# First stage of a hybrid encoder layer: orders written out for three engines, four open value accumulators, constant matmuls between the real ones

## The chip, the cores and the metric

One core of a Trainium2 chip runs the whole layer in one launch. The metric is the device time of that launch in microseconds (us), the median of several runs. The engines are named as the profile names them: PE is TensorE (PEld its weight loads), ACT is ScalarE, DVE is VectorE, POOL is GpSimd, SP issues most of the DMAs.

## What is computed

A layer of width 1024 over 512 positions: a layer norm, one wide projection `w_in` (8 window heads, and three groups of 8 dilated heads, each with q, k and v), two kinds of attention mixed by their softmax denominators, an output projection, a cross attention to a 256-row memory, and a gated feed-forward part, each followed by a residual layer norm. The change touches only the start:

```
h <- LayerNorm(x, ln_in_g, ln_in_b)                 # x is 512 x 1024
z <- h @ w_in;  qa, ka, va, qb, kb, vb = split(z)
# the change: LayerNorm of x, and vb of the first dilated group (512 columns from VB = 3840)
```

## The kernel before, in words

**Precision.** A product of two float32 matrices is made of three matmuls in a faster 32-bit format (`F32R`): each operand is split into a high part (`hi`, a cast on ScalarE, L139) and a low part (`lo = raw - hi`, a subtraction, L141, on VectorE or GpSimd), and hi*hi, hi*lo and lo*hi are summed in PSUM. Weights come by DMA into the tile `raw` (three buffers), and their parts lie in `hi` and `lo` (six buffers each). The transposed activations lie in `Thi` and `Tlo`.

**First stage** (L235 to L358). Rows are taken in four blocks of 128 (`h[0]` to `h[3]`; blocks 0 and 1 lie in tile `oA`, 2 and 3 in `oB`). For each block VectorE takes mean and variance (`stats`, L282, `moments`, L116 and L118), GpSimd the inverse root (L112), VectorE applies gain (L331, `gin` is the gain broadcast) and then shift (L333, `bt` is the bias broadcast, made by two matmuls from the row `brow`), TensorE turns the block in eight 128x128 pieces (`hi_both`, L294), ScalarE casts them to `Thi` (L299), VectorE subtracts for `Tlo` (L327). ScalarE also writes alpha*h to DRAM for the residual (`oW`, L302, L303). Then come the 24 matmuls of that block's values (8 pieces of depth, three products each) into one PSUM tile `g`, copied to `vt` (L341). So the values need 4 x 24 = 96 matmuls of 512 columns; their weights are four pairs of rows, `wv0[0]` to `wv0[3]`, and I call them w0 to w3, and the blocks of the input x0 to x3. Before the first real matmul TensorE multiplies a tile of ones 18 times (`WARM`, L250).

**Order.** Only VectorE's order in this stage is as written (`manual_schedule`). The list `ORDER` sets the order of the loads: x0, gain, w0, x1, w1, w2, x2, x3, w3. w3 must wait for one of the three `raw` buffers. A scheduler with a timeline of its own orders the other engines, and interleaves what follows with the end of the stage.

**What follows.** The projections of the dilated heads: each is a chunk of 24 matmuls into a PSUM tile `g` (two buffers), then a rotation by position (`rope`): VectorE multiplies by `rc` and swaps lanes (L366, L367), GpSimd multiplies by `rsn` and adds (L368, L369). `rc` and `rsn` are sines from ScalarE (L356, L358) of angles that VectorE reduces to one turn (L348 to L357). After three chunks, k0, q0 and the window keys `ka`, comes the first attention item A0, whose first matmuls are `s<-x`. From there on the order of TensorE is written out (`manual_schedule` again).

The memory's rows are also normalised early: `mem_load` (L715, L720) loads gain, bias and rows, and VectorE does the norm on `oB` between the angles.

Of the kernel before, what the change touches and what calls it, by code (L numbers as in the profile page):

```python
# [17 lines left out]
P = 128  # L18
# [30 lines left out]
]  # L49

MEM_AT = (2, 0)
KX = 6
WARM = 18
ORDER = (4, 8, 0, 5, 1, 2, 3, 6, 7)
CI, CF, CS, CMA, CM1, CM3 = 0, 128, 129, 130, 514, 770
CW = 898

# [16 lines left out]
def hymba_layer(ctx: ExitStack, tc: tile.TileContext, A, cst_d, out):  # L74
# [25 lines left out]
    def halves(t):  # L100
        return [t[:, i * 512 : (i + 1) * 512] for i in range(2)]
# [57 lines left out]
    def mm(o, l, r, first, last):  # L159
        nc.tensor.matmul(o, l, r, start=first, stop=last)  # L160
# [26 lines left out]
    def ps_tile(tag, bufs, shape=None):  # L187
        return gpool.tile(shape or [P, 512], F32, tag=tag, bufs=bufs, name=tag)
# [48 lines left out]
    def load_x(b):  # L237
        nc.sync.dma_start(h[b], x2[b * P : (b + 1) * P, :])
# [3 lines left out]
    nc.vector.memset(ones_t, 1.0)  # L242
    brow = wpool.tile([1, D], F32, tag="gb", bufs=2, name="brow")
    nc.sync.dma_start(brow, A["ln_in_b"].partition_broadcast(1))
    ps = ps_tile("t", 1)
    for i in range(WARM):
        mm(ps[:, 0:P], ones_t, ones_t, i == 0, i == WARM - 1)
    sbt = s_tile()
    bt = [sbt[:, n, :] for n in range(2)]
    for n in range(2):  # L250
        mm(bt[n], ones_t[0:1, :], brow[:, n * 512 : (n + 1) * 512], True, True)
    gin = wpool.tile([P, D], F32, tag="gb", bufs=2, name="gin")
    gt = halves(gin)
    wv0 = []
    for u in ORDER:
        if u < 4:
            wv0.append(w_rows(w_in, 2 * u, 2, VB, 512, nc.gpsimd))
        elif u < 8:
            load_x(u - 4)
        else:  # L260
            nc.sync.dma_start(gin, A["ln_in_g"].partition_broadcast(P))
# [14 lines left out]

    hT = T_pair()

    def stats(b):
# [3 lines left out]
        return moments(st)  # L283

    def hi_both(b):
        if b % 2:
            both = s_tile()
            pss = [both[:, i, :] for i in range(2)]
        else:
            pss = [ps_tile("t", 1), ps_tile("o", 1)]  # L290
        out = []
        for i in range(2):
            for k in range(4):
                nc.tensor.transpose(  # L294
                    pss[i][:, k * P : (k + 1) * P], h[b][:, i * 512 + k * P : i * 512 + (k + 1) * P], ident
                )
            hi = hT[0][:, 4 * i : 4 * i + 4, b * P : (b + 1) * P]
            src = pss[i].rearrange("p (k t) -> p k t", k=4)
            nc.scalar.copy(hi, src)  # L299
            out.append((src, hi))  # L300
        ah = oW[:, 2 * (b % 2) : 2 * (b % 2) + 2, :].rearrange("p a f -> p (a f)")
        nc.scalar.activation(ah, h[b], AF.Copy, scale=ALPHA)  # L302
        nc.scalar.dma_start(h_dram[b * P : (b + 1) * P, :], ah)  # L303
        return out

    vt = mkv.tile([P, NB, 512], F32, tag="vm", name="vt")

    def w_v(b, ps, part):
        if b > 1:
            gemm_tm(ps, wv0, hT, blk(b - 1), KX * part, (KX, KD)[part])  # L310
            return
        for k in range(KD):
            whi, wlo = (t[:, k % 2, :] for t in wv0[k // 2])
            if part == 0:
                mm(ps, hT[0][:, k, 0:P], whi, k == 0, False)
                mm(ps, hT[1][:, k, 0:P], whi, False, False)
            else:
                mm(ps, hT[0][:, k, 0:P], wlo, False, k == KD - 1)

    with tc.manual_schedule(engines={nc.vector.engine}):  # L320
        pend = []
        for b in range(NB + 1):
            if b < NB:
                mv, rs = stats(b)
            for i, (ps, hi) in enumerate(pend):
                lo = hT[1][:, 4 * i : 4 * i + 4, (b - 1) * P : b * P]
                nc.vector.tensor_tensor(lo, ps, hi.bitcast(F32), ALU.subtract)  # L327
            if b < NB:
                th = halves(h[b])
                for i in range(2):  # L330
                    nc.vector.scalar_tensor_tensor(th[i], th[i], mv[:, 0:1], gt[i], ALU.subtract, ALU.mult)  # L331
                for i in range(2):
                    nc.vector.scalar_tensor_tensor(th[i], th[i], rs, bt[i], ALU.mult, ALU.add)  # L333
            if b:
                ps = g_tile()
                w_v(b, ps, 0)
            if b < NB:
                pend = hi_both(b)
            if b:
                w_v(b, ps, 1)  # L340
                nc.scalar.copy(vt[:, b - 1, :], ps)  # L341

        rc = cpool.tile([P, S], F32, name="rc")
        rsn = cpool.tile([P, S], F32, name="rsn")
# [366 lines left out]
    def mem_load(b):  # L711
        if b == 0:
            for v in ("mem_ln_g", "mem_ln_b"):
                t = wpool.tile([P, D], F32, tag="gb", bufs=2, name="gm")
                nc.sync.dma_start(t, A[v][0].partition_broadcast(P))  # L715
                gbm.append(halves(t))
            mx = oB[:, 2:4, :].rearrange("p a f -> p (a f)")
        else:
            mx = wpool.tile([P, D], F32, tag="hi", bufs=6, name="mx")
        nc.sync.dma_start(mx, A["mem"].rearrange("o s d -> (o s) d")[b * P : (b + 1) * P, :])  # L720
        mxs[b] = mx

    def mem_T(b, mx):
# [473 lines left out]
```

## Time and profile before

| | |
|---|---|
| median of 3 runs | 975.44 us (975.24 to 977.02) |
| profiled execution, its own time | 976.09 us |
| its span, first to last instruction | 974.0 us |
| busy in the span | PE 95%, DVE 50%, ACT 38%, POOL 21% |
| mean granted TensorE clock | 0.978 of full |

The span is split into 40 slices on the page, so the first stage with the first projections is about the first three of them. A row of the timeline gives start, duration, engine, line, what is written from what, and in brackets the idle time of the engine ahead of it with what ended it. Matmuls overlap: the distance of two starts is what one costs, not its duration. A row of the table by stretches gives a stretch, its length, the busy time of each engine with its instructions, then the granted clock, DMA share and GB/s.

### The profile page before, as it was taken

How to read it: one execution, taken by the hardware profiler on the slowest of the kernel's cores; microseconds unless marked ns; L12 is line 12 of the kernel's file. 1: busy time of each engine (PE TensorE's matmuls, PEld its weight loads, DVE VectorE, ACT ScalarE, POOL GpSimd, SP SyncE). 2: the span in 40 equal slices, each digit the busy share in tenths (PEclk: the TensorE clock that was granted, in tenths of full speed). 3: DMA queues.
4: the chain of work that ended last, by engine and by line, in shares of the span. 5: the costliest groups of instructions: out<-in, count | busy, mean ns of one | idle time of the engine just before them, and what ended most of it. 6: DMA issues, size and time to landing. Idle time of an engine off the chain costs nothing.

```text
span 974.0 us, 12289 instructions
## 1 busy us (share of the span) xinstructions
PE 926.4 (95%) x4825; PEld 770.1 (79%) x4825; DVE 490.2 (50%) x866; ACT 366.4 (38%) x645; POOL 206.4 (21%) x135
## 2 busy tenths in 40 slices
PE   7989999999998899899899997999999999999996
PEld 5777887788776698688887786988888888788885
DVE  6683334524444564749435648454434443333346
ACT  3453444335544557322334512433323332232310
POOL 4253114511443232424541043000000000000001
PEclk7999999999999899999999997999999999999999
DMA  9542032313221227432531034233333333223201
GB/s 320 163 152 65 22 108 66 87 44 108 66 66 47 62 88 214 132 102 58 155 119 44 1 87 130 70 107 104 92 101 95 97 98 98 98 87 108 87 22 65
DMA packets 117066, 93.33 MB, mean 96 GB/s; under 512 B 12471, under 2 KB 100751, under 8 KB 117008
## 3 DMA queue, kind: packets, MB, share of 16 engines
q1 hardware_dynamic: 115106, 90.33, 30.6%
q10 hardware_dynamic: 1902, 2.21, 0.7%
q8 instruction: 38, 0.62, 0.3%
q14 instruction: 20, 0.16, 0.1%
HBM read 88.34 MB, written 4.19 MB: 95 GB/s over the span
## 4 chain that ended last, share of the span: by engine, by line
PE 59%; DVE 5%; ACT 2%; issue 2%; POOL 1%; DMA 0%; DVEq 0%; ACTq 0%; POOLq 0%
PE g L160 25%; PE s L160 15%; PE acc L160 12%; PE t L160 3%; PE o L160 2%; DVE h L129 1%; POOL lo L141 0%; ACT hi L139 0%; DVE lo L141 0%; PE s L206 0%; ACT pu L596 0%; PE t L505 0%; DMA raw<-in_w_xq_dram 0%; PE o L513 0%; DVE ka L704 0%
## 5 line engine op out<-in xcount | busy, mean ns | idle before, releaser
L139 ACT CAST hi<-raw 128x1024 fp32r<-128x1024 f32 x148 | 155.3, 1050 | 249.2 <-PE g L160 161.9
L141 DVE TENSOR_TENSOR lo<-raw,hi 128x1024 fp32r<-128x1024 f32 x114 | 141.7, 1244 | 147.8 <-ACT hi L139 145.7
L141 POOL TENSOR_TENSOR lo<-raw,hi 128x1024 fp32r<-128x1024 f32 x34 | 84.8, 2506 | 121.5 <-ACT hi L139 120.9
L112 POOL TENSOR_TENSOR rs<-ve,mhalf 128x1 f32<-128x1 f32 x18 | 15.6, 868 | 416.6 <-DVE ve L118 416.6
L160 PE MATMUL g<-Thi,hi 128*128 128x512 f32 x240 | 97.6, 407 | 2.1 <-DVE zs L367 2.1
L160 PE MATMUL g<-Thi,lo 128*128 128x512 f32 x240 | 97.0, 404 | 0.0
L160 PE MATMUL g<-Tlo,hi 128*128 128x512 f32 x240 | 96.7, 403 | 0.0
L160 PE MATMUL g<-Ulo,hi 128*128 128x512 f32 (+1 forms) x248 | 91.9, 371 | 1.1 <-DVE Ulo L212 1.0
L160 PE MATMUL g<-Uhi,hi 128*128 128x512 f32 (+1 forms) x248 | 91.7, 372 | 0.6 <-ACT Uhi L211 0.5
L160 PE MATMUL g<-Uhi,lo 128*128 128x512 f32 (+1 forms) x248 | 91.5, 369 | 0.0
L368 POOL TENSOR_TENSOR zs<-zs,rsn 128x512 f32<-128x512 f32 x29 | 57.5, 1983 | 148.4 <-DVE zs L367 148.4
L160 PE MATMUL g<-hi,Thi 128*128 128x512 f32 x200 | 82.7, 414 | 0.5 <-ACT Thi L299 0.3
L160 PE MATMUL g<-hi,Tlo 128*128 128x512 f32 x200 | 81.3, 408 | 1.8 <-DVE Tlo L327 1.8
L160 PE MATMUL g<-lo,Thi 128*128 128x512 f32 x200 | 78.5, 398 | 0.0
L160 PE MATMUL s<-Uhi,hi 128*128 128x512 f32 (+1 forms) x192 | 71.3, 371 | 0.0
L160 PE MATMUL s<-Ulo,hi 128*128 128x512 f32 (+1 forms) x192 | 71.3, 371 | 0.0
L160 PE MATMUL s<-Uhi,lo 128*128 128x512 f32 (+1 forms) x192 | 71.3, 371 | 0.0
L160 PE MATMUL acc<-hi 128*128 128x512 f32 x176 | 68.6, 390 | 0.8 <-DVE act L1117 0.8
L160 PE MATMUL acc<-hi,lo 128*128 128x512 f32 x176 | 68.5, 389 | 0.0
L160 PE MATMUL acc<-lo,hi 128*128 128x512 f32 x176 | 68.5, 389 | 0.0
L160 PEld LDWEIGHTS g<-Thi,hi 128*128 128x128 f32 x240 | 45.8, 191 | 13.5 <-DVE zs L367 2.9
L160 PEld LDWEIGHTS g<-Ulo,hi 128*128 128x128 f32 x248 | 48.8, 197 | 8.7 <-DVE Ulo L212 1.6
(259 smaller groups left out, 1737.4 us busy)
## 6 DMA issues: line engine op xcount, KB each, us to landing
raw<-in_w_in_dram SPq DMA_DIRECT2D x38, 512.0 KB, 3.9
raw<-in_w_gate_dram SPq DMA_DIRECT2D x22, 512.0 KB, 3.8
raw<-in_w_up_dram SPq DMA_DIRECT2D x22, 512.0 KB, 3.9
raw<-in_w_down_dram SPq DMA_DIRECT2D x22, 512.0 KB, 3.3
raw<-in_w_xk_dram SPq DMA_DIRECT2D x8, 512.0 KB, 3.9
raw<-in_w_xv_dram SPq DMA_DIRECT2D x8, 512.0 KB, 3.3
raw<-in_w_xq_dram SPq DMA_DIRECT2D x8, 512.0 KB, 4.1
raw<-in_w_xo_dram SPq DMA_DIRECT2D x8, 512.0 KB, 3.3
```

Of the source, the lines that this page charges most:

```text
L112: nc.gpsimd.tensor_tensor(out_, in_, mhalf, ALU.pow)
L129: nc.vector.scalar_tensor_tensor(th[i], th[i], rs, bt[i], ALU.mult, ALU.add)
L139: nc.scalar.copy(hi, raw)
L141: (eng or nc.vector).tensor_tensor(lo, raw, hi.bitcast(F32), ALU.subtract)
L160: nc.tensor.matmul(o, l, r, start=first, stop=last)
L368: nc.gpsimd.tensor_tensor(sh, sh, rsn, ALU.mult)
```

## The change

Only the first stage is rewritten; line numbers after it are moved by 127, those of the helpers ahead of it by -2.

- **Orders.** TensorE, VectorE and ScalarE all run the stage in the order in which the code stands.
- **Four accumulators.** The values of the four blocks are summed in four PSUM regions that are open at once (`vps`: two `g` tiles and the two halves of an `s` tile). The products hi*hi (`hh`), Tlo*hi (`lh`) and Thi*lo (`hl`) are issued apart.
- **Weights.** The low parts of all four pairs w0 to w3 move from GpSimd to VectorE (`v_lo`). w3 is loaded as two halves into two tiles of another pool, `x`, ahead of x2 and x3.
- **Sums.** Blocks 2 and 3 take their sums on ScalarE (`sums`: part 0 the sum, part 1 the sum of squares about the mean, each one activation over 1024 columns with `accum_out`), and VectorE makes of them the negated mean and the variance (`neg_mean`, `root`).
- **Constants.** The 18 matmuls of ones become 10 ahead of the bias matmuls and 13 behind them, and `busy(3)`, `busy(4)`, `busy(3)` stand at three places between real ones.
- **Transposes** of every block go through the PSUM tiles `t` and `o` (one buffer each).
- **Memory loads** keep the program's order, so they stand behind the weights of the next value group.

```diff
-WARM = 18
-ORDER = (4, 8, 0, 5, 1, 2, 3, 6, 7)
+WARM = (10, 13)
...
-    for u in ORDER:
-        if u < 4:
-            wv0.append(w_rows(w_in, 2 * u, 2, VB, 512, nc.gpsimd))
...
+    def v_raw(i):
...
+        if i < 3:
+            raw = [wpool.tile([P, 2, 512], F32, tag="raw", bufs=3, name="raw")]
+            nc.sync.dma_start(raw[0], src)
         else:
+            raw = [xpool.tile([P, 1, 512], F32, tag="x", bufs=12, name="raw") for _ in range(2)]
+            for k in range(2):
+                nc.sync.dma_start(raw[k], src[:, k : k + 1, :])
...
+    def v_lo(i):
+        for raw, hi, lo in v_parts(i):
+            nc.vector.tensor_tensor(lo, raw, hi.bitcast(F32), ALU.subtract)
+
+    load_x(0)
+    nc.sync.dma_start(gin, A["ln_in_g"].partition_broadcast(P))
+    v_raw(0)
+    load_x(1)
+    for i in range(1, 4):
+        v_raw(i)
+    load_x(2)
+    load_x(3)
...
+    def sums(b, part):
...
+        if part == 0:
+            nc.scalar.activation(junk, h[b], AF.Copy, accum_out=sm)
...
         else:
+            nc.scalar.activation(junk, h[b], AF.Square, bias=LN["nm", b], accum_out=sm)
...
-    with tc.manual_schedule(engines={nc.vector.engine}):
...
+    with tc.manual_schedule(engines={nc.tensor.engine, nc.vector.engine, nc.scalar.engine}):
+        spare = ps_tile("t", 1)
+
+        def busy(n, ps=None):
+            for _ in range(n):
+                mm((spare if ps is None else ps)[:, 0:P], ones_t, ones_t, True, True)
+
+        busy(WARM[0])
+        for n in range(2):
+            mm(bt[n], ones_t[0:1, :], brow[:, n * 512 : (n + 1) * 512], True, True)
+        busy(WARM[1])
+        vps = [g_tile(), g_tile()]
+        two = s_tile()
+        vps += [two[:, i, :] for i in range(2)]
...
+        busy(3, vps[1])
+        hh(0, 0, 1)
+        busy(4, vps[1])
+        hh(0, 2, 3)
+        lh(0, 0, 1, 2, 3)
...
+        sums(2, 0)
+        neg_mean(2)
+        sums(3, 0)
+        turn(1)
+        t_hi(1)
+        v_lo(0)
...
+        turn(3)
+        t_hi(3)
+        v_lo(3)
+        t_lo(3)
+        for b in range(3):
+            hl(b, 6, 7)
+            nc.scalar.copy(vt[:, b, :], vps[b])
+        hh(3, *all_k)
+        hl(3, *all_k)
+        lh(3, *all_k)
+        spill(2)
+        spill(3)
+        nc.scalar.copy(vt[:, 3, :], vps[3])
...
-                nc.sync.dma_start(t, A[v][0].partition_broadcast(P))
+                tc.keep_in_program_order(nc.sync.dma_start(t, A[v][0].partition_broadcast(P)))
```

`turn(b)` is the eight transposes of a block, `t_hi` and `t_lo` its two parts, `gain` and `shift` the two steps of the norm, `spill` the write of alpha*h. Three places of the orders follow; a row is a line of the kernel, the operation, what it writes from what, its shape and how often it stands there in a row.

ScalarE, from the casts of the value weights on to block 2. `hi<-raw` is a cast of weights, `Thi<-` the cast of a turned block, `oW<-` the write of alpha*h. Before:

```order
L139 CAST hi<-raw 128x1024
L302 ACTIVATE oW<-oA 128x1024
L303 DMA h_dram<-oW 128x1024
L299 CAST Thi<-s 128x4x128
L139 CAST hi<-raw 128x1024
L299 CAST Thi<-s 128x4x128
L139 CAST hi<-raw 128x1024 x2
L302 ACTIVATE oW<-oB 128x1024
```

Now, from the sums of blocks 2 and 3 (`zs,sm<-oB`) on; `L137 CAST hi<-raw` is the cast of the weights of k0:

```order
L313 ACTIVATE zs,sm<-oB 128x1024 x2
L354 CAST Thi<-t 128x4x128
L354 CAST Thi<-o 128x4x128
L316 ACTIVATE zs,sm<-oB,nm 128x1024 x2
L363 ACTIVATE oW<-oA 128x1024
L137 CAST hi<-raw 128x1024
L364 DMA h_dram<-oW 128x1024
L354 CAST Thi<-t 128x4x128
L354 CAST Thi<-o 128x4x128
```

The casts of block 1 moved behind the two sums, and a cast of the next stage's weights stands ahead of block 2's.

TensorE, at the transposes of block 2. `g<-hi,Thi` and the like are value matmuls (a written `g` or `s` is the accumulator), `t<-cst` and `o<-cst` transposes. Before, where each block's 24 stand alone:

```order
L294 MATMUL t<-cst,oB 128x128 x4
L294 MATMUL o<-cst,oB 128x128 x4
L160 MATMUL g<-hi,Thi 128x512
L160 MATMUL g<-lo,Thi 128x512
L160 MATMUL g<-hi,Tlo 128x512
L160 MATMUL g<-hi,Thi 128x512
L160 MATMUL g<-lo,Thi 128x512
```

Now, from the transposes of block 2 on, with `lo` the low part of the weights:

```order
L347 MATMUL t<-cst,oB 128x128 x4
L347 MATMUL o<-cst,oB 128x128 x4
L158 MATMUL g<-lo,Thi 128x512 x8
L158 MATMUL s<-hi,Thi 128x512 x8
L158 MATMUL s<-hi,Tlo 128x512 x8
L158 MATMUL s<-lo,Thi 128x512 x4
L158 MATMUL g<-lo,Thi 128x512 x4
L158 MATMUL s<-lo,Thi 128x512 x2
L347 MATMUL t<-cst,oB 128x128 x4
L347 MATMUL o<-cst,oB 128x128 x4
L158 MATMUL g<-lo,Thi 128x512 x4
L158 MATMUL s<-lo,Thi 128x512 x2
```

The matmuls with low weight parts of blocks 0 and 1 stand behind the transposes of block 2, and those of all three blocks around the transposes of block 3.

ScalarE at the end of the stage: the copy of block 3's values, the casts of the next weights and the two sines (`rsn`, `rc`). Before:

```order
L139 CAST hi<-raw 128x1024 x3
L341 COPY vt<-g 128x512
L139 CAST hi<-raw 128x1024
L356 ACT_TABLE_LOAD
L356 ACTIVATE rsn<-zs,cst 128x512
L139 CAST hi<-raw 128x1024
L358 ACTIVATE rc<-zs,halfpi 128x512
```

Now:

```order
L363 ACTIVATE oW<-oB 128x1024
L364 DMA h_dram<-oW 128x1024
L137 CAST hi<-raw 128x1024 x3
L468 COPY vt<-s 128x512
L483 ACT_TABLE_LOAD
L483 ACTIVATE rsn<-zs,cst 128x512
L485 ACTIVATE rc<-zs,halfpi 128x512
```

Three casts of weights now stand together ahead of the last copy, and the sines' table load directly behind it.

More of the change, by code (lines that the diff above doesn't have):

```diff
@@ L277, in hymba_layer @@
     hT = T_pair()
+    vt = mkv.tile([P, NB, 512], F32, tag="vm", name="vt")
+    LN = {}
     def stats(b):
@@ L293, in hi_both, with shift, turn @@
+    def shift(b):
+        th = halves(h[b])
+        for i in range(2):
+            nc.vector.scalar_tensor_tensor(th[i], th[i], LN["rs", b], bt[i], ALU.mult, ALU.add)
+    def turn(b):
+        LN["T", b] = []
+        for i in range(2):
+            ps = ps_tile(("t", "o")[i], 1)
             for k in range(4):
                 nc.tensor.transpose(
-                    pss[i][:, k * P : (k + 1) * P], h[b][:, i * 512 + k * P : i * 512 + (k + 1) * P], ident
+                    ps[:, k * P : (k + 1) * P], h[b][:, i * 512 + k * P : i * 512 + (k + 1) * P], ident
@@ L301, in hi_both, with spill @@
+    def spill(b):
         ah = oW[:, 2 * (b % 2) : 2 * (b % 2) + 2, :].rearrange("p a f -> p (a f)")
@@ L303, in hi_both @@
         nc.scalar.dma_start(h_dram[b * P : (b + 1) * P, :], ah)
[L304 to L318, printed above, removed]
```

144 lines of the change are left out of this document (100 added, 44 removed).

## The prediction

> **What bounds the kernel now.** I read the page first (span, busy shares, clock row), then a table by stretches, then the timeline of the first 70 us.
>
> ```profile
> span 974.0 us, 12289 instructions
> PE 926.4 (95%) x4825; PEld 770.1 (79%) x4825; DVE 490.2 (50%) x866; ACT 366.4 (38%) x645; POOL 206.4 (21%) x135
> PEclk7999999999999899999999997999999999999999
> ```
>
> TensorE is busy 95% of the span, nobody else above 50% (PEld runs beside PE). Idle TensorE time and time at a low clock are thus the whole price of a stage, and the clock row's lowest digits include the first slice.
>
> ```profile
> 0.00:12.20 12.20, 10.02 (x49) 7.79 (x49) 6.07 (x15) 3.59 (x4) 2.69 (x6) 1.00 0.82 270
> 12.20:25.86 13.66, 9.40 (x25) 6.93 (x26) 10.46 (x16) 7.30 (x10) 8.88 (x6) 0.50 0.99 350
> 25.86:44.00 18.14, 16.42 (x78) 12.73 (x77) 11.68 (x19) 6.34 (x10) 0.68 (x2) 1.00 0.67 187
> 44.00:67.70 23.70, 21.07 (x92) 16.79 (x90) 19.47 (x28) 10.18 (x11) 11.91 (x7) 1.00 0.46 146
> 67.70:160.00 92.30, 92.28 (x506) 76.66 (x507) 38.11 (x104) 43.25 (x102) 27.54 (x21) 1.00 0.25 69
> ```
>
> The columns are the stretch, its length, PE, PEld, DVE, ACT and POOL busy, the clock, DMA share, GB/s. From 12.20 to 25.86 TensorE has half its clock and only 25 records. Behind 67.70, where A0 starts, it is busy 92.28 of 92.30 us. So A0's start is the mark: what is done earlier there moves the end.
>
> ```profile
> 1.14 6.29 PE L160 MATMUL t<-zs 128*128 128x128 f32 x36 [1.14 <-DVE zs L242]
> 7.37 1.98 PE L160 MATMUL s<-brow,zs 1*128 1x512 f32 x4
> 9.44 1.41 DVE L333 SCALAR_TENSOR_TENSOR oA<-oA,rs,s 128x512 f32<-128x512 f32 x2 [0.62 <-PE s L160]
> 10.25 0.66 PE L294 MATMUL t<-cst,oA 128*128 128x128 f32 x4 [0.90 <-DVE oA L333]
> 13.09 0.38 SPq L154 DMA_DIRECT2D raw<-in_w_in_dram  x1
> 14.54 4.65 DVE L331 SCALAR_TENSOR_TENSOR oA<-oA,mv,gin 128x512 f32<-128x512 f32 x2
> 19.90 1.12 PE L294 MATMUL s<-cst,oA 128*128 128x128 f32 x4 [1.71 <-DVE oA L333]
> ...
> 67.72 1.95 PE L160 MATMUL s<-x 64*64 64x128 f32 x20 [0.54 <-POOL x L369]
> ```
>
> Three faults show. w3 is asked for only at 13.09. Block 1's gain takes 4.65 us while GpSimd makes low parts beside it. Its transposes come at 19.90 and cost 1.12 us, against 0.66 for block 0's at full clock.
>
> **The change part by part.** Unit prices first.
>
> ```profile
> 1.14:5.36 4.22, 4.22 (x20) 4.22 (x20) 0.29 (x1) 1.28 (x1) 0.00 (x0) 1.00 0.68 194
> 5.36:7.36 2.00, 2.00 (x18) 1.88 (x17) 1.35 (x4) 0.00 (x0) 0.49 (x1) 1.00 0.97 308
> 27.39 0.40 PE L160 MATMUL g<-hi,Tlo 128*128 128x512 f32 x1
> 29.89 0.39 PE L160 MATMUL g<-lo,Thi 128*128 128x512 f32 x1
> ...
> 9.14 1.04 ACT L139 CAST hi<-raw 128x1024 fp32r<-128x1024 f32 x1 [4.63 <-DMA raw<-in_w_in_dram]
> 29.69 1.06 ACT L302 ACTIVATE oW<-oB 128x1024 f32<-128x1024 f32 x1 [3.42 <-DVE oB L333]
> L547 ACT ACTIVATION_READ_ACCUMULATOR pu<-pu,stT 128x1 f32 x32 | 6.0, 187 | 0.0
> 33.52 0.59 ACT L299 CAST Thi<-t 128x512 fp32r<-128x512 f32 x1
> 27.79 1.21 DVE L141 TENSOR_TENSOR lo<-raw,hi 128x1024 fp32r<-128x1024 f32 x1
> 34.15 0.69 DVE L327 TENSOR_TENSOR Tlo<-t,Thi 128x512 fp32r<-128x512 f32 x1 [1.86 <-ACT Thi L299]
> 35.35 1.41 DVE L331 SCALAR_TENSOR_TENSOR oB<-oB,mv,gin 128x512 f32<-128x512 f32 x2
> ```
>
> A constant matmul is two passes: 4.22/20 = 0.21 us each to 5.36, about 0.11 behind it, so the full clock came near 5.4. From 27.39 to 29.89 lie 11 steps: a 512-column matmul costs 0.227 us (at half clock 0.427). A gain alone on VectorE is 1.41.
>
> *Loads.* Their order decides when weights and rows are there.
>
> ```profile
> 3.38 2.06 SPq L154 DMA_DIRECT2D raw<-in_w_in_dram  x2
> DMA to landing us min/median/max: 3.9/6.5/8.2
> ...
> 6.90 0.85 SPq L238 DMA_DIRECT2D oB<-in_x_dram  x2
> DMA to landing us min/median/max: 7.7/8.1/8.4
> ```
>
> The upper pair is of `raw` (w1, w2 and later weights), the lower of x2 and x3. w2 is issued near 5.1 and lands near 13.3; x2 at 6.9+7.7 = 14.6, x3 at 7.4+8.4 = 15.8: one 512 KB piece each 1.3 us. w3 now takes x2's place: w3 14.6, x2 15.9, x3 17.1.
>
> *Start and constants.* 10 constants: 20 x 0.21 = 4.3, to 5.4. Bias: four passes of 0.43, to 7.1, so block 0's shift loses its 0.62 wait. 13 constants: 26 x 0.11 = 2.9, to 10.0, where the transposes start (10.25 before). The other ten stand where TensorE waits for a cast: block 0's at 11.2 to 13.3, block 1's at 17.8; I cost them at nothing, and at most 10 x 0.22 = 2.2 without that cover.
>
> *Block 0.* ScalarE casts the block to 11.8, then w1, w2, w3 as they land, the last to 15.4; the last four matmuls follow: 16.4. VectorE's gain for block 1 is 1.41, not 4.65, and its shift is done at 16.2; transposes 16.4 to 17.7.
>
> *Block 1.* Here the change adds waits to ScalarE's queue: the sums of x2 (15.9, 1.06 + 0.19 = 1.25) and x3 (17.1 to 18.3) stand ahead of block 1's casts. No row has a 1024-column sum: it lies between 1.06 with a free read-out and 1.44 with one that takes twice as long; I take the sum of the two nearest rows. Two of the four are on the path, so 0.4 us either way. So those run 18.3 to 19.5, TensorE waits 1.1 us, and block 1's 16 high-part matmuls end at 22.6. VectorE has the four low parts now, 4 x 1.21 = 4.8 us, but none of the two blocks' statistics.
>
> *Block 2.* Squares on ScalarE to 20.6, then on VectorE gain 1.41 (22.0), w1's low part 1.21 (23.2), half a shift 0.7 (23.9). TensorE waits 1.3 us more; transposes to 25.2.
>
> *From there* TensorE has 34 matmuls, the transposes of block 3 (1.3), 6, then 22 of k0, block 3's 24, and 26 that end k0 and q0: 112 x 0.227 + 1.3 = 26.7, to 51.9. Beside it VectorE finishes block 3's shift near 30, so its transposes at 33 don't wait; low parts of k0 and q0 (2.4) and then of block 3 are done by 35.4, as k0 starts.
>
> *Rotation.*
>
> ```profile
> 53.25 1.28 ACT L356 ACT_TABLE_LOAD   x1
> 55.98 0.72 ACT L356 ACTIVATE rsn<-zs,cst 128x512 f32<-128x512 f32 x1 [1.45 <-DVE zs L355]
> 60.06 0.68 DVE L366 TENSOR_TENSOR zs<-g,rc 128x512 f32<-128x512 f32 x1
> 60.67 0.72 DVE L367 STREAM_SHUFFLE zs<-g 128x512 f32<-128x512 f32 x1
> 61.44 0.50 PE L160 MATMUL g<-Thi,hi 128*128 128x512 f32 x1 [2.11 <-DVE zs L367]
> 61.53 1.29 POOL L368 TENSOR_TENSOR zs<-zs,rsn 128x512 f32<-128x512 f32 x1 [9.38 <-DVE zs L367]
> 62.90 2.16 POOL L369 TENSOR_TENSOR x<-zs 128x512 f32<-128x512 f32 x1
> 84.56 0.69 DVE L476 COPY va<-t 128x512 f32<-128x512 f32 x1 [6.59 <-PE t L475]
> ```
>
> Before, the third chunk waits 2.11 us at 61.44 for k0's PSUM buffer, since the rotation starts late. Now the sines stand behind three weight casts and block 3's copy, which TensorE releases at 44.5 and 45.9: casts to 47.5, copy 48, table 49.3, two sines 50.7, VectorE 0.68 + 0.72 to 52.2. TensorE waits 0.3 to 0.6 there, 24 matmuls (5.45) bring it to 57.8. GpSimd does k0 and q0 from 52.2 in four steps of 1.29 to 2.16, near 58. So A0 starts at 58.1 against 67.72.
>
> *Memory norm.* It moves behind A0's reductions on VectorE and costs some 4.5 us there (two statistics, 1.41 + 1.41, the rest). VectorE's idle 6.59 us ahead of 84.56 hides it; without that cover it would be 4.5 late.
>
> **Sum.** 67.7 - 58.1 = 9.6 us. On the profiled execution's own time: 976.09 - 9.6 = 966.5; that run lies 0.65 above the median of 975.44, so 965.8. My chain carries some 30 steps of handing over between engines at an estimated 0.05 us, so it may be short by 1; later falls of the clock (the 8 and the 7 in the clock row) shift against the program and may add or save one piece at half clock, 1.5 to 2 us by estimate.
>
> **The rivals.**
>
> *The full clock comes late.* In the timeline it came near 5.4, about as the 10th constant ends. Had it not come then, the bias would cost 3.4 and 13 constants 5.5 us: transposes at 14.4, not 10.0. ScalarE's waits for w1 to x3 take up some 1.6 of this, leaving 2.7: 968.5. For it speaks that only 10 constants stand ahead of bias matmuls of one row; against it, that this run's clock rose within them. The Trainium skill, "TensorE: Matmul & The Clock Gate", Part 1, has the full clock follow a whole busy window of about 3.4 us, the windows running free of the kernel's start: a run of 4.3 us holds a whole one in a quarter of the phases by estimate, so by that rule alone 968.5 would be the forecast and not 965.8. The rise near 5.4 agrees with it for this one phase; whether a one-row matmul counts as busy no run here shows. From the rows, I give it 22%.
>
> *ScalarE stands behind k0's weights.* Their cast is queued ahead of block 2's casts; the load can start only when VectorE has w0's low part (18.4) and is wanted at 22.7. With the 3.9 us of the row it is hidden; with the median 6.5 or the 8.2, 1.7 to 3.4 us are lost: 967.5 to 969.2. The long ones fall in the stretch of DMA share 0.99, and at 18.4 all early loads have landed, so I take the short end. A fall of the clock near 25, after 2.7 us in which TensorE has only transposes, would cost as much (one or two pieces of 3.4 us at half clock). 13% together.
>
> *Slower: the clock stays at half.* Before, it fell at 12.2 behind transposes and stayed for 13.66 us although TensorE was busy for 9.40 of them. Each matmul at half clock costs 0.2 more; 48 of them eat the 9.6 us, all 118 up to block 3's end would give 965.8 + 23.6 = 989. Against it: from 25.2 on TensorE has 112 matmuls without a wait, and before the clock returned after some 3 us of such work. 3%.
>
> *Hidden anyway.* A0 comes earlier but something fixed holds the rest: 975.4. The 92.28 of 92.30 speaks against it. 3%.
>
> **How the numbers follow.** The likeliest case, 965.8 with its own range 963 to 967.5, has 57%; the late clock 22%, ScalarE's wait or a fall 13%, hidden 3%, slower 3%, and 2% for a larger gain than I see. The range of 962.5 to 970.5 leaves out the last three. A measurement here can tell 0.2%, 2 us, from no change: faster by more 0.93, within 0.03, slower 0.04.
>
> **What the profile after would show.** `s<-x` starts near 58; full clock from about 5 on without a stretch like 12.20 to 25.86; block 1's gain 1.4 us; TensorE waiting about 1 us each for block 1's casts and block 2's shift; the 2.11 us at the third chunk below 1. Wrong would make me: transposes of block 0 behind 12, a cast of k0's weights that waits over 2 us with block 2's casts behind it, or TensorE waits behind A0 that weren't there.

## The result and the profile after

The changed kernel takes 970.79 us (median of 20 runs, 969.66 to 975.6), the kernel before 976.65 us in the same series (20 runs from 974.93). Two disturbed runs are in no ratio: one of the kernel before (1052.2 us), and the profiled one of the repeat in experiment 1 (4691.44 us), which thus left no second profile to read. The ratio is 0.9949, 95% interval 0.9935 to 0.9962: faster by 5.0 us by the ratio and by 5.9 between the medians, about half of the 9.6 us forecast, and the time is 0.3 us outside the range. The profiled execution took 973.17 us.

The page after, its span, its busy shares and its clock row:

```profile
span 971.3 us, 12351 instructions
PE 929.1 (96%) x4855; PEld 774.5 (80%) x4855; DVE 486.9 (50%) x867; ACT 370.5 (38%) x654; POOL 199.9 (21%) x131
PEclk9999999999999899899999997999999999999999
```

The 7 that stood for the first slice is a 9. The table by stretches of the changed kernel (the columns are those of the table of before), cut at block 0's and block 2's transposes, at the third chunk and at A0:

```profile
0.00:12.10 12.10, 10.90 (x51) 9.34 (x51) 6.16 (x15) 2.33 (x2) 0.75 (x5) 0.86 0.82 270
12.10:25.05 12.95, 11.53 (x69) 9.86 (x69) 10.26 (x19) 11.54 (x18) 2.00 (x2) 1.00 0.63 223
25.05:53.22 28.17, 27.71 (x129) 22.50 (x129) 18.35 (x29) 14.01 (x19) 6.30 (x4) 1.00 0.59 171
53.22:61.32 8.10, 5.70 (x24) 4.39 (x24) 6.86 (x10) 4.65 (x5) 7.89 (x4) 1.00 0.80 233
```

From 12.10 to 25.05 TensorE now has the full clock and 69 records, 20 of them constants, where before it had half the clock and 25 in about the same time. (The clock column counts the time ahead of the clock's first record, 4.87 here, as full, though a constant takes 0.21 us there as before.) The holes that are left: a clock of 0.86 ahead of 12.10, 1.42 us idle at block 2, and 2.40 us in the last stretch, in which GpSimd is busy for 7.89 of 8.10 us. The timeline of TensorE, the rows that answer to those shown of before:

```profile
1.14 4.26 PE L158 MATMUL t<-zs 128*128 128x128 f32 x20 [1.14 <-DVE zs L240]
5.33 1.98 PE L158 MATMUL s<-brow,zs 1*128 1x512 f32 x4
7.24 4.80 PE L158 MATMUL t<-zs 128*128 128x128 f32 x26
12.10 0.66 PE L347 MATMUL t<-cst,oA 128*128 128x128 f32 x4
...
25.05 0.63 PE L347 MATMUL t<-cst,oB 128*128 128x128 f32 x4 [1.42 <-issue]
...
53.22 0.47 PE L158 MATMUL g<-Thi,hi 128*128 128x512 f32 x1 [0.39 <-DVE zs L494]
61.32 0.87 PE L158 MATMUL s<-x 64*64 64x128 f32 x10 [2.40 <-POOL x L496]
```

A0 starts at 61.32 (forecast 58.1, before 67.72). The 26 constant records behind the bias take 4.80 us, not 2.9. And behind A0, the kernel before and then the changed one, from A0 to the end:

```profile
67.72:974.00 906.28, 869.53 (x4585) 725.87 (x4585) 442.50 (x792) 338.98 (x613) 182.28 (x116) 0.98 0.29 87
```

```profile
61.32:971.00 909.68, 873.30 (x4585) 728.43 (x4585) 445.29 (x798) 338.00 (x612) 182.93 (x117) 0.98 0.29 88
```

The same 4585 matmuls take 3.4 us longer. So the profiled execution was short of its forecast by 3.2 us ahead of A0 and by 3.4 to 3.7 behind it.

### The profile page after: what moved, and what is told of

Read it like the earlier page. It is cut to its first block, busy times and chain, and to the rows that moved or that the text cites. A ratio compares the mean times of both kernels' runs of the same rounds, so it can differ in the third digit from the quotient of the medians.

```text
span 971.3 us, 12351 instructions
## 1 busy us (share of the span) xinstructions
PE 929.1 (96%) x4855; PEld 774.5 (80%) x4855; DVE 486.9 (50%) x867; ACT 370.5 (38%) x654; POOL 199.9 (21%) x131
## 4 chain that ended last, share of the span: by engine, by line
PE 59%; DVE 5%; ACT 2%; issue 2%; POOL 1%; DMA 0%; DVEq 0%; ACTq 0%; POOLq 0%
PE g L158 25%; PE s L158 15%; PE acc L158 12%; PE t L158 3%; PE o L158 2%; DVE h L127 1%; POOL lo L139 0%; ACT hi L137 0%; DVE lo L139 0%; PE s L204 0%; ACT pu L723 0%; PE t L632 0%; DMA raw<-in_w_xq_dram 0%; PE o L640 0%; DVE ka L831 0%
## 5 line engine op out<-in xcount | busy, mean ns | idle before, releaser
L137 ACT CAST hi<-raw 128x1024 fp32r<-128x1024 f32 x144 | 151.1, 1051 | 243.7 <-PE g L158 152.6
L139 POOL TENSOR_TENSOR lo<-raw,hi 128x1024 fp32r<-128x1024 f32 x30 | 76.0, 2549 | 123.2 <-ACT hi L137 122.6
L158 PE MATMUL g<-hi,Thi 128*128 128x512 f32 x184 | 73.1, 407 | 0.2 <-DVE h L1117 0.2
L158 PE MATMUL g<-lo,Thi 128*128 128x512 f32 x184 | 71.7, 401 | 0.0
L158 PE MATMUL g<-hi,Tlo 128*128 128x512 f32 x184 | 71.2, 399 | 0.0
L493 DVE TENSOR_TENSOR zs<-g,rc 128x512 f32<-128x512 f32 x29 | 20.0, 690 | 70.8 <-PE g L158 35.2
```

Source lines behind the costliest of these rows:

```text
L137: nc.scalar.copy(hi, raw)
L139: (eng or nc.vector).tensor_tensor(lo, raw, hi.bitcast(F32), ALU.subtract)
L493: nc.vector.tensor_tensor(zc, ps, rc, ALU.mult)
```

## The experiments

All medians are of several runs, with the ratio to the kernel before in the same series and its interval. "A0" is the start of `s<-x`. Each median is to be compared with the changed kernel's 970.8.

### 1. The bias over 128 rows (bias128), and the changed kernel again (a_again)

```diff
-    brow = wpool.tile([1, D], F32, ...)
-    nc.sync.dma_start(brow, A["ln_in_b"]...)
+    brow = wpool.tile([P, D], F32, ...)
+    nc.gpsimd.memset(brow, 0.0)
     load_x(0)
+    nc.sync.dma_start(brow[0:1, :], A["ln_in_b"]...)
-    mm(bt[n], ones_t[0:1, :], brow[...], True, True)
+    mm(bt[n], ones_t, brow[...], True, True)
```

> The changed kernel once more, for a second profile and more times. Theory 'clock': the granted clock rises after the first constants, falls again while the one-row bias matmuls run (they don't count as work for the clock), and how much of the 13 constants then runs at half clock depends on where the clock's 3.41 us steps fall in this run: transposes of block 0 between 9.7 and 14.4 us, 12.1 in the first profile. Theory 'GpSimd': the first attention item waits for GpSimd's rotation of q0 (2.40 us at 61.3 in the first profile) in every phase, here 1.5 to 2.6 us. Rival: the wait of 2.4 us was an accident of that run and is below 0.6 here. Time 970 to 975, as the 20 runs.

> The bias row is laid into a tile of 128 rows, the others zero, and the two bias matmuls contract over all 128 rows instead of one; the result is the same. Theory 'clock': the array counts as busy all along, so the clock, once up, does not fall before 12 us, the 26 passes of the 13 constants take 0.11 us each (2.9 in all, not 4.8), and block 0's transposes start near 10.1, not 12.1; the first attention item comes up to 2 us earlier than in the first profile of the changed kernel (59.3 against 61.3), and the median falls by 1 to 2 us. Rival: the clock falls for another reason (always in the window after its first rise): same fall, transposes near 12, no change in time.

Again: 970.69 us over five runs, ratio 0.9943 (0.9925 to 0.996). What was expected of its profile has no answer from this run; but in the five other profiles that keep this rotation and this place of A0 (bias128, fill, lo_pool, stats_dve, no_busy) A0 waits 2.34 to 2.37 us, so the 2.40 was no accident of one run. With 128 rows: 969.74 us, 0.992 (0.9907 to 0.9934); the two intervals overlap. TensorE's timeline with 128 rows:

```profile
1.14 3.84 PE L158 MATMUL t<-zs 128*128 128x128 f32 x20 [1.14 <-DVE zs L240]
6.46 1.95 PE L158 MATMUL s<-brow,zs 128*128 128x512 f32 x4 [1.48 <-DMA brow<-in_ln_in_b_dram]
8.26 3.06 PE L158 MATMUL t<-zs 128*128 128x128 f32 x26
11.38 0.66 PE L348 MATMUL t<-cst,oA 128*128 128x128 f32 x4
```

The same 26 constants take 3.06 us in place of 4.80. The clock's records show why: its stretches are multiples of 3.41 us, which I call windows. In the changed kernel the clock rose at 4.87, fell at 8.28 and rose again at 11.69. With 128 rows it rose at 4.0 and stayed up for 58 us. The first window behind the rise, in the changed kernel and then with 128 rows:

```profile
4.87:8.28 3.41, 3.41 (x18) 2.04 (x17) 1.91 (x5) 0.00 (x0) 0.55 (x1) 1.00 0.95 319
```

```profile
4.00:7.41 3.41, 1.93 (x12) 1.29 (x11) 2.55 (x6) 0.51 (x1) 0.55 (x1) 1.00 0.98 310
```

TensorE is busy throughout the first, but for more than half of it (5.33 to 7.24) with matmuls over one row, and the clock fell at its end. It is busy for only 1.93 us of the second, and the clock stayed. So the one-row matmuls don't keep the clock up: this is the mechanism of my first rival, in another place. About 1.7 us come back at the constants; the row now lands later (a wait of 1.48), so block 0's transposes gain 0.7 and A0 0.8 (60.54). The median gains 1.0, which the intervals can't tell from nothing.

### 2. The rotation of k0 and q0 on VectorE (rope_dve), and both (bias_rope)

```diff
-        nc.gpsimd.tensor_tensor(sh, sh, rsn, ALU.mult)
-        nc.gpsimd.tensor_tensor(view[1](dest), ...)
+        eng = nc.vector if rn[0] < 3 else nc.gpsimd
+        eng.tensor_tensor(sh, sh, rsn, ALU.mult)
+        eng.tensor_tensor(view[1](dest), ...)
```

> The rotation's product and sum for k0 and q0 run on VectorE instead of GpSimd (four instructions). Theory 'GpSimd': its four steps of 1.3 to 2.3 us in a row, stretched by VectorE's low parts beside them, are what the first attention item waits for; on VectorE they take 0.6 to 0.7 each and the wait is gone (below 0.4 us), the item starts 2 to 2.4 us earlier (about 59), and the fall of the clock near 63 (it costs 1.3 us) goes too: 2 to 3.5 us off the median, 967 to 969. Rival: VectorE is as late, or TensorE then waits as long for something behind it: 970 to 971.

> Both edits. If the two costs add up, the first attention item starts near 57.3 and the median is 965.5 to 968. If they hide each other (the item waits for one chain only), it is no better than the better of the two alone.

970.05 us, 0.9935 (0.9915 to 0.9954), and 969.33 us, 0.9918 (0.9899 to 0.9937). The waits of TensorE with the rotation on VectorE:

```profile
60.13 1.95 PE L158 MATMUL s<-x 64*64 64x128 f32 x20 [1.52 <-DVE x L497]
```

and VectorE's timeline there:

```profile
54.76 0.74 DVE L494 STREAM_SHUFFLE zs<-g 128x512 f32<-128x512 f32 x1
55.39 2.34 DVE L139 TENSOR_TENSOR lo<-raw,hi 128x1024 fp32r<-128x1024 f32 x2
57.65 0.69 DVE L496 TENSOR_TENSOR zs<-zs,rsn 128x512 f32<-128x512 f32 x1
58.25 1.22 DVE L139 TENSOR_TENSOR lo<-raw,hi 128x1024 fp32r<-128x1024 f32 x1
59.39 0.69 DVE L497 TENSOR_TENSOR x<-zs 128x512 f32<-128x512 f32 x1
```

The wait fell from 2.40 to 1.52 only, because the scheduler put three low parts of later weights (3.5 us) between q0's swap and its sum. So most of the wait moved from GpSimd's queue to VectorE's. The fall of the clock near 63 is gone in both profiles, but neither time can be told from that without the edit (970.05 against 970.8, 969.33 against 969.74 of bias128): the 2 to 3.5 us of the theory did not come, and the two edits together ended above their 965.5 to 968.

### 3. A0 twelve matmuls later (later)

```diff
-        ready[key] = now[0] + LAG
+        ready[key] = now[0] + (LAG if rn[0] > 2 else 36)
```

> The changed kernel with A0 let in 36 matmuls behind k0 and q0 and not 24, so that 12 matmuls of the fourth chunk, which stood behind A0's group, stand ahead of it; no other row of TensorE moves. Theory (A0 waits 2.40 us for GpSimd's four rotation steps, which end at 61.3, and nothing else is late): the 12 matmuls (2.7 us) run in the wait, which falls to 0 to 0.2; the fall of the clock near 63 goes too (1.3 us); median 966.5 to 968.5. Rival (the fourth chunk's weight is as late as the rotation, or the later parts of the chain bind): the wait stands ahead of the 12 matmuls, 970 to 971.

968.74 us, 0.9908 (0.989 to 0.9926). TensorE's row of A0:

```profile
61.48 1.95 PE L158 MATMUL s<-x 64*64 64x128 f32 x20
```

A0 starts at the same time, but waits for nothing, and 12 matmuls of the fourth chunk lie behind it already; the fall near 63 is gone. The theory holds: 2.0 us by the medians, though 968.74 lies 0.2 above its range. Nothing else was late at A0.

### 4. Who makes GpSimd's steps long (lo_wait)

The steps that A0 waits for, on GpSimd in the changed kernel, and the low parts on VectorE beside them:

```profile
53.22 1.31 POOL L495 TENSOR_TENSOR zs<-zs,rsn 128x512 f32<-128x512 f32 x1 [0.72 <-DVE zs L494]
54.60 2.16 POOL L496 TENSOR_TENSOR x<-zs 128x512 f32<-128x512 f32 x1
56.73 2.34 POOL L495 TENSOR_TENSOR zs<-zs,rsn 128x512 f32<-128x512 f32 x1
59.14 2.13 POOL L496 TENSOR_TENSOR x<-zs 128x512 f32<-128x512 f32 x1
```

```profile
54.21 1.39 DVE L139 TENSOR_TENSOR lo<-raw,hi 128x1024 fp32r<-128x1024 f32 x1
56.69 1.23 DVE L139 TENSOR_TENSOR lo<-raw,hi 128x1024 fp32r<-128x1024 f32 x1 [1.09 <-ACT hi L137]
58.07 2.07 DVE L139 TENSOR_TENSOR lo<-raw,hi 128x1024 fp32r<-128x1024 f32 x1 [0.16 <-ACT hi L137]
```

The edit holds these three low parts back until q0's sum has ended:

```diff
-        (eng or nc.vector).tensor_tensor(lo, raw, hi..., ALU.subtract)
+        part = (eng or nc.vector).tensor_tensor(lo, raw, hi..., ALU.subtract)
+        # three low parts on VectorE, those behind the third chunk's:
+        tc.add_manual_dep(part.ins, <q0's sum>, Sync)
```

> The changed kernel with the three low parts that VectorE makes behind q0's product and shuffle held back until GpSimd has ended q0's sum. Theory (GpSimd's steps are long because VectorE's low parts run beside them): the four steps, 1.31, 2.16, 2.34 and 2.13 us in the changed kernel, come down to some 1.3 each, the last ends at 58.6 to 59, TensorE's wait of 2.40 falls to 0 to 0.4 and the fall of the clock near 63 goes: 967.5 to 969; a new wait of the fourth chunk for its low part up to 1 us. Rival (the steps have their lengths by themselves, or by what they read): still 8 us from 53.2 to 61.3, the wait of 2.4 stays and the low parts come 2 us later on top: 971 to 973.

974.92 us, 0.9977 (0.9967 to 0.9988). GpSimd, with the low parts held back:

```profile
52.60 1.30 POOL L505 TENSOR_TENSOR zs<-zs,rsn 128x512 f32<-128x512 f32 x1 [0.71 <-DVE zs L504]
53.98 1.29 POOL L506 TENSOR_TENSOR x<-zs 128x512 f32<-128x512 f32 x1
55.23 1.30 POOL L505 TENSOR_TENSOR zs<-zs,rsn 128x512 f32<-128x512 f32 x1
56.61 1.30 POOL L506 TENSOR_TENSOR x<-zs 128x512 f32<-128x512 f32 x1
```

TensorE in the same run:

```profile
58.23 1.95 PE L168 MATMUL s<-x 64*64 64x128 f32 x20
...
66.10 0.33 PE L645 MATMUL t<-cst,pu 128*128 128x128 f32 x1 [1.61 <-ACT pu L687]
67.96 0.97 PE L645 MATMUL t<-cst,pu 128*128 128x128 f32 x3 [1.53 <-ACT pu L687]
```

On the mechanism the theory was right to a tenth: the four steps take 1.30 each, and A0 starts at 58.23 with no wait, where the prediction had put it (58.1). Of the 3.1 us that A0 comes earlier, 0.6 are this execution's start, in which the clock did not fall (GpSimd's first step at 52.60 and not 53.22). On the time it was wrong: 974.92 lies above both ranges. The low parts now stand ahead of A0's reductions on VectorE, A0's transposes wait 1.61 and 1.53 us for the exponentials, the clock falls for 3.4 us at 68.0, and by 72 us into the span TensorE is 0.5 us behind the changed kernel. So VectorE's 3.5 us of low parts must run beside something here; the cheap way is to let GpSimd be slow and give TensorE other work, as in experiment 3. The Trainium skill, "SBUF — State Buffer", section "Who interferes with whom", says that a VectorE instruction with two inputs in SBUF and a GpSimd instruction that reads SBUF exclude each other, and that the one that comes second waits for the whole of the other. The trace agrees: the steps are 1.3 or about 2.15 with nothing between (2.34 where two low parts touch one step), and the third low part itself takes 2.07 in place of 1.22.

### 5. Parts undone: low parts on GpSimd (lo_pool), statistics on VectorE (stats_dve), no constants between (no_busy)

```diff
# lo_pool, in v_lo
-            nc.vector.tensor_tensor(lo, raw, ...)
+            nc.gpsimd.tensor_tensor(lo, raw, ...)
# stats_dve: sums(2, ·), neg_mean(2), root(2) -> stats(2); the same for block 3
# no_busy
-        busy(3, vps[1])
-        busy(4, vps[1])
-        busy(3, vps[2])
```

> The changed kernel with the low parts of the four value weights made by GpSimd again, where VectorE made them. Theory (two engines working beside each other on these rows slow each other, as in the kernel before, where the gain took 4.65 us beside GpSimd's low parts): block 2's gain and shift, 2.8 us alone, stretch to 6 or more and TensorE's wait for block 2 grows from 1.4 to 4 or more; A0 2.5 to 4 us later than 61.3, 973 to 975. Rival (VectorE had too much to do, and each low part taken off it is 1.22 us won): A0 at 60 to 61.3, 969.5 to 971.

> The changed kernel with the statistics of blocks 2 and 3 made by VectorE's own statistics instructions (1.29 + 0.21 + 0.15 us for a block) and no sums or squares on ScalarE. Theory (VectorE is what TensorE waits for at block 2): VectorE's queue grows by 1.65 us ahead of block 2's gain, while ScalarE's casts of block 1 start 1.2 us earlier; the wait for block 2 (1.42) grows to 2 to 3, A0 0.5 to 1.5 us later, 971 to 972.5. Rival (ScalarE binds, its 5 us of sums stand ahead of every cast): A0 1 us earlier, 969 to 970.

> The changed kernel without the ten constant matmuls between block 0's and block 1's matmuls (2.2 us of TensorE). Theory (they hold the clock up): in the windows of 3.4 us between 11.7 and 22 TensorE then has work for only half the time, the clock falls for one to three windows, each costs 1 to 1.4 us, A0 1 to 4 us later: 972 to 975. Rival (they cost time or do nothing): 970 to 971, the clock row as it was.

Low parts on GpSimd: 973.67 us, 0.9981 (0.9964 to 0.9998), 2.9 more; block 2's transposes come at 26.80. The theory's direction holds, its sizes don't: block 1's gain takes 3.56 and block 2's 2.07 in place of 1.41, but the wait is 2.01 in place of 1.42, not 4 or more, and A0 comes 1.8 later (63.08), not 2.5 to 4. By the ratios as they stand, over half of the gain is gone without this part.

Statistics on VectorE: 972.55 us, 0.9953 (0.9939 to 0.9967). The wait at block 2 is 2.58, as the theory had it, and in this profile the clock falls at 25.9; A0 comes at 63.76. The ratio can't be told from the changed kernel's, so what the sums on ScalarE are worth in time isn't shown.

No constants between: 972.01 us, 0.9947 (0.9929 to 0.9965), no difference that can be told, and the clock did not fall from 13.6 to 64.8. The ten constants show no effect here; that is one profile, whose clock rose late. This profile shows something else, the forecast's first rival as it was written:

```profile
1.14 4.63 PE L158 MATMUL t<-zs 128*128 128x128 f32 x20 [1.14 <-DVE zs L240]
5.70 3.78 PE L158 MATMUL s<-brow,zs 1*128 1x512 f32 x4
9.41 5.15 PE L158 MATMUL t<-zs 128*128 128x128 f32 x26
14.62 0.66 PE L347 MATMUL t<-cst,oA 128*128 128x128 f32 x4
```

Here the clock rose only at 13.6: bias 3.78 us, transposes at 14.62 (the rival said 3.4 and 14.4), A0 at 63.77. The code up to block 0's transposes is the changed kernel's. Where the windows lie differs from execution to execution: in eight profiles with the one-row bias and ten constants ahead of it the first rise came at 4.2 to 5.5 in six, at 6.5 in one (lo_wait) and at 13.6 in one. The six fell again at 7.6 to 8.9. The one at 6.5 did not fall: 1.5 us of its window were one-row matmuls, less than half, and block 0's transposes came at 11.23.

### 6. Both repairs, with the row's wait covered (bias_later)

Experiments 1 and 3 together, and `WARM = (16, 5)` in place of `(10, 13)`.

> The changed kernel with the bias matmuls over 128 rows (as in the run of that name), 16 constant matmuls ahead of them, so that TensorE doesn't wait for the row, and 5 behind; and A0 let in 36 matmuls behind k0 and q0. Theory: the two gains add up: the row's wait of 1.48 us is covered, transposes of block 0 near 9.3 in place of 12.1, and the start 0.7 to 1.7 us shorter, A0's wait gone: 966 to 968. Rival (the early transposes only wait for w1 to w3, and the gain of the start was the clock's alone): 967.5 to 968.7. Rival two (with another start the clock may rise a window later, at 9 to 13): 969 to 971.

964.75 us, 0.9873 (0.9855 to 0.989): 12.4 us below the kernel before, 6.0 below the changed one and 1.2 below the theory's range, the fastest of all. The table by stretches, cut at the same events:

```profile
0.00:9.53 9.53, 8.33 (x46) 7.19 (x46) 4.41 (x12) 2.18 (x2) 1.71 (x6) 1.00 0.79 254
9.53:23.91 14.38, 11.93 (x68) 9.96 (x69) 12.16 (x23) 12.00 (x19) 2.00 (x2) 1.00 0.75 270
23.91:52.09 28.18, 27.72 (x129) 22.51 (x129) 18.36 (x29) 14.05 (x19) 6.30 (x4) 1.00 0.55 163
52.09:60.43 8.34, 8.34 (x37) 6.65 (x37) 6.62 (x9) 3.76 (x4) 8.00 (x5) 1.00 0.83 234
```

Transposes at 9.53 and block 2 at 23.91; from 52.09 to A0 TensorE has no idle time. With the 12 matmuls moved (2.7 us) A0 stands 3.6 us earlier in the work than in the changed kernel. Between the two profiled executions, 964.84 and 973.17 us, the other 4.7 lie behind A0, where this one has 23.9 us at half clock and the changed kernel 34.1.

### 7. The low clock behind A0 (fill, before_fill, best, fill592)

In eight profiles of kernels whose code behind A0 is the same, the time from A0 to the end goes with the time at half clock behind A0, read from the clock's records (the stretch that runs into the end is left out, and so is lo_wait, 37.5 and 914.6, where three low parts moved behind A0):

| kernel | half clock behind A0, us | A0 to end, us |
|---|---|---|
| bias_rope | 20.5 | 904.6 |
| rope_dve | 23.9 | 906.4 |
| before | 27.3 | 906.3 |
| stats_dve | 27.3 | 907.3 |
| no_busy | 27.3 | 907.5 |
| lo_pool | 30.7 | 908.5 |
| bias128 | 34.1 | 908.9 |
| changed | 34.1 | 910.0 |

A line through them has a slope of 0.34 us for each us (correlation 0.96), 1.2 us for each window of 3.41. The executions of one kernel go the same way: over 65 of the kernel before, time and granted clock have a correlation of -0.86. And the traces show the places. The lead of the changed kernel, from the starts of the same TensorE record in both traces, is 6.4 us at A0 and 4.8 behind its fall at 62.9, which the kernel before doesn't have. It is still 4.8 at 314, 4.4 behind falls near 300 and 330 that both have, 2.0 behind three falls at 377 to 404 where the kernel before has one, 3.5 behind a fall at 473 that only the kernel before has, and 2.6 from 608 on, where transposes stand in another order and TensorE waits 0.68 and 0.22 us that the kernel before doesn't wait. So some 2.9 of the lost 3.8 us go where the clock is low, and 0.9 at that wait.

The first try to take these falls away put constants into the later waits:

```diff
+    def fill(o, n):
+        for _ in range(n):
+            mm(o, ident, ident, True, True)
# ahead of the memory's transposes 13 and 19, of the statistics' 5, of the `rh` pairs 2 and 5, in to_T 17
```

> The changed kernel with constant matmuls (128x128, two passes, 0.22 us at full clock) put on TensorE into its later waits: 13 and 19 ahead of the memory transposes (waits of 3.31 and 4.64 us), 5 ahead of the statistics' transposes (1.28), 2 and 5 ahead of the pairs that read `rh` (0.53, 1.38, 1.38) and 17 ahead of the last transposes of the second norm (4.20). Theory: behind A0 the time hangs on the stretches at half clock; over the five profiles so far A0 to end is 904.6, 906.4, 906.3, 908.9 and 910.0 us with 20.5, 23.9, 27.3, 34.1 and 34.1 us at half clock. The 30.6 us from 301 to 602 go, A0 to end falls by 0.3 to 0.4 of that, 9 to 12 us, to 898 to 901, and the median from 970.8 to 959 to 962. Rival, the matmuls in the waits only stand in the way: no gain, or 0.2 to 0.5 us lost for each place, 971 to 974.

> The kernel before with the same constant matmuls at the same places. Theory (what is missing behind A0 is the place of the half-clock stretches, not the work): A0 stays at 67.7, A0 to end is that of the changed kernel with the same matmuls within 1 us (898 to 901), and the two medians differ by the 6.4 us of A0 less the fall near 63 (1.3), so by 5 to 6.4. Rival (the change itself makes something behind A0 slower, by a transfer or a buffer): A0 to end is 2.5 to 4 us shorter here than in the changed kernel with the matmuls, and the medians differ by 2.5 to 4.

> The changed kernel with all of this together: the bias row in a zeroed 128-row tile loaded over ScalarE's queue, so that its matmuls contract over 128 rows, 7 constant matmuls behind them and not 13; A0 let in 36 matmuls behind k0 and q0; the constant matmuls in the later waits. Theory: transposes of block 0 near 9.9, the clock up from 4 on, no wait of A0; start 1 us, A0 3 to 3.7 us, later stretches 9 to 12 us: 955 to 958. Rivals: the early transposes wait for w1 to w3 anyway, so that the start brings 0: 956 to 959; the places interfere and only the later stretches count: 959 to 962.

979.76 us (1.0024, 1.0013 to 1.0036), 985.58 us (1.0083, 1.0068 to 1.0099) and 976.06 us (0.9985, 0.9973 to 0.9998). The first two are 9 us slower than the same kernels without the constants, and the third is 14 us above the highest of its ranges, which neither theories nor rivals had. TensorE in the changed kernel with the constants, its constants and the memory's transposes:

```profile
294.86 3.07 PE L159 MATMUL t<-cst 128*128 128x128 f32 x26
297.77 0.60 PE L864 MATMUL t<-cst,oB 128*128 128x128 f32 x4
302.07 0.79 PE L864 MATMUL t<-cst,oB 128*128 128x128 f32 x4 [1.88 <-DVE x L869]
```

The wait is at the second four transposes, and my constants stood at the first, where they only took their 3 us; the 17 went to a block that doesn't wait. So these three runs don't settle what the low clock costs: in the first two the time at half clock behind A0 fell by 6.8 us, but the constants took more. They do say that the kernel before and the changed one differ by the same with the constants as without (5.8 us by the medians), as before_fill's theory had it. In the two profiles A0 to the end is 2.8 us shorter in the kernel before (913.7 against 916.5), as its rival had it, with 6.8 us less at half clock. In the third, the row went over ScalarE's queue, came at 7.3, and the clock rose at 13.4.

The second try put 17 constants exactly into the longest wait, 4.2 us near 588, on top of experiment 6:

```diff
+            tc.keep_in_program_order(nc.tensor.matmul(ps[:, 0, 0:P], ident, ident, ...))
# to_T of blocks 1 to 3 written behind block 3's product, 17 constants ahead of block 1's
```

> The kernel of the run before with the bias over 128 rows, 16 and 5 constant matmuls and the later A0, and 17 constant matmuls (3.7 us at full clock) directly ahead of the transposes of the second norm's block 1, behind the last matmul of its product, where TensorE waits 4.2 us for VectorE and the clock then is at half for 10.2 us in nearly all profiles. Theory (behind A0 the time hangs on the stretches at half clock, 0.35 us for each us by the spread of nine profiles): the 10.2 us go, 3 to 3.6 us shorter, 961 to 962. Rival (the matmuls only fill time and the half clock costs little there, since TensorE waits for other engines in it): 964 to 965.5.

967.69 us, 0.9895 (0.9879 to 0.9912). From 583 to 600, without the constants (experiment 6) and then with them:

```profile
583.00:600.00 17.00, 13.57 (x78) 12.77 (x79) 14.00 (x24) 4.27 (x7) 3.05 (x3) 0.70 0.54 164
```

```profile
583.00:600.00 17.00, 13.64 (x99) 12.44 (x97) 14.31 (x25) 3.67 (x6) 4.21 (x3) 0.90 0.62 185
```

The half clock shrank from 10.2 to 3.4 us there, as meant, and the time did not: it is no shorter than experiment 6's (the intervals overlap), and 967.69 lies above the rival's range too. The traces show two effects. From the last matmul of the product (580.26 in experiment 6, 581.41 here) until the next 48 matmuls (`g<-U`) and the 16 transposes that stand among or behind them are through, 18.9 us pass in experiment 6 and 17.5 here. But the edit also moved those transposes behind the 48 matmuls, and then TensorE waits 0.68 and 0.23 us for ScalarE and VectorE, which it doesn't in experiment 6. So 6.8 us less at half clock brought some 1.3 us here, less than the slope of the table, since TensorE waits for other engines in part of this stretch, and the order took most of it back. No experiment removes the low clock behind A0 alone. That most of the 3.4 us is lost there is read from the traces; why the falls come where they do in one execution and not in another stays open.

## Why the prediction was wrong

**Right.** That A0's start carries the gain; block 1's gain of 1.41, and the wait of 2.11 at the third chunk down to 0.39. From block 2's transposes to the end of the 112 matmuls it had 28.0 us (23.9 to 51.9), and 27.8 were measured (25.05 to 53.22 less the wait of 0.39). The sums on ScalarE took 1.06 to 1.17 with 0.18 to 0.20 for the read-out, where it had 1.25. k0's weights delayed ScalarE's queue by 0.36. The memory norm cost nothing: the lead over the kernel before stays at 4.7 to 4.8 us from 68 to 300. The fall near 25 was seen in one profile (statistics on VectorE), not in the changed kernel's.

**The step "start and constants"** failed: 13 constants took 4.80 us, not 2.9, and block 0's transposes came at 12.10, not 10.0, which the prediction itself had named as a sign of being wrong (behind 12). The rival had the right mechanism (a one-row matmul may not count as work) but only as a late rise; what came in most profiles was a rise, a fall at about 8 and a second rise. Of the 2.1 us only 1.15 reach block 2 (25.05 against 23.9), because waits that the prediction had on the way vanished: ScalarE casts w1 to w3 in a row (13.75 to 16.8) and waits for none of them, and TensorE doesn't wait the forecast 1.1 us for block 1's casts. Experiment 6 gives the 1.15 back: 23.91. By the rule of the Trainium skill, "TensorE: Matmul & The Clock Gate", Part 1, a busy window of about 3.4 us brings the full clock, and the windows run free of the kernel's start. The first rises, at 4.2 to 13.6 with the same code ahead of them, agree with the second half. The rise at 4.0 in bias128 came behind a window (0.59 to 4.0) that was busy for 2.86 us, so it need not be a whole one. That one-row matmuls don't count is not in that rule; experiment 1 shows it.

**The step "rotation"** failed most. I took GpSimd's four steps about as before (1.29, 2.16, 1.29, 1.28: 6.0 us). They took 7.94, since the earlier stage brings VectorE's low parts of the next weights right beside them. Of the span "1.29 to 2.16" that I quoted I priced little more than the lower end. TensorE was ready at 58.92 (57.8 forecast, the 1.1 from the start again) and A0 waited to 61.32. Experiment 3 shows that this wait with the fall behind it was worth 2.0 us; experiment 4 shows its cause, and that taking the cause away gives a wait in its place.

**The term "1.5 to 2 us" for later falls** was too small for the profiled execution: 3.4 us behind A0, with two falls more than before. In the 20 runs of the changed kernel 13 lie at 969.66 to 971.23 (granted clock 0.981 to 0.984) and 7 at 972.8 to 975.6 (0.977 to 0.983); the profiled one is of the upper group.

By the medians the miss is 5.0 us. The forecast started from a median of three runs, 975.44; in the series of the result the same kernel takes 976.65, so 1.2 of the 5.0 are no fault of the working, and without them the time would have lain inside the range: that it lies outside by 0.3 is in part bad luck. The two steps above failed all the same. Ahead of A0 the profiled execution misses 3.2 us, 1.1 by the start and the rest by the rotation. The two repairs bring 6.0 us by the medians (964.75), but in the profiles only 3.6 of the 8.3 us lie ahead of A0. How much of the rest is where the clock's windows happen to fall stays open.

## What to carry to other kernels

When a stage is pulled forward, price the engines behind it by what will then run beside them, not by the durations they had: that a low part on VectorE makes a GpSimd step 2.16 us long and not 1.29 was in the profile, on one step of four. A wait at a known place was cheaper here to cover with work that was ready (12 matmuls of the next chunk) than to remove. Put a filler into the row where the trace shows the idle time, with its order pinned, or it costs its whole length.

## What was unexpected of the hardware

- Matmuls that contract over one row don't hold the clock: a window of 3.41 us, busy throughout and for more than half with them, ended in a fall (six profiles, 7.6 to 8.9); over 128 rows there was none in four, though TensorE was busy for only 1.93 us of the window in one.
- A GpSimd product or sum of 128x512 takes 1.3 us alone and 2.15 beside one of VectorE's subtractions with two inputs in SBUF, and a gain on VectorE 1.41 us, or 2.07 and 3.56 beside GpSimd's.
- A window at half clock costs what runs in it: near 63, on busy matmuls, 3.41 us took 1.6 us from the lead; near 590, where TensorE waits for others in part of the time, 6.8 us less of it brought some 1.3.
